# A decoder layer on one core: first weights in halves, the first norm without GpSimd, and additions to x by transfers

## The chip, the core and the metric

The kernel runs on one core of a Trainium2 chip. Five engines work side by side: TensorE (PE, matrix products into PSUM), VectorE (DVE), ScalarE (ACT), GpSimd (POOL) and SyncE (SP, which only issues transfers). Transfers run on 16 DMA engines. The metric is the device time of one execution in microseconds; the time of a kernel is the median of its runs.

## The reference

One decoder layer in float32, 512 tokens by 1024 channels:

```python
x = x + 0.5 * swiglu(rms_norm(x, g_ffn1), w_ffn1_gate, w_ffn1_up, w_ffn1_down)
h = rms_norm(x, g_mix)
q, k, v, u, mq = split(h @ w_in)
# sliding-window attention, conv module, cross-attention into 256 memory tokens
x = x + concat([y_attn, y_conv, y_mem]) @ w_out
x = x + 0.5 * swiglu(rms_norm(x, g_ffn2), w_ffn2_gate, w_ffn2_up, w_ffn2_down)

def rms_norm(x, g):
    return x * rsqrt(mean(x * x, axis=-1) + 1e-6) * g
def swiglu(x, w_gate, w_up, w_down):
    return (silu(x @ w_gate) * (x @ w_up)) @ w_down
```

The hidden width of each feed-forward block is 2816.

## The kernel before

x stays in on-chip memory, transposed: `x[:, d]` is channel block d (128 channels on the partitions, 512 tokens along each), d = 0 to 7. A hidden tile f (0 to 21) is 128 hidden channels.

**Products.** Each float32 product is made of three matmuls over rounded parts (`mm3`, lines 337 to 339): high part of the weights by high part of the data, high by low, low by high. So each weight tile and each data tile is split first: ScalarE copies it to the rounded type (`whi`, `xh`, `hh`), and VectorE subtracts that from the original (`wlo`, `xl`, `hl`). `Weights` does this for the weights: `load_to` issues the transfer of a 128x1024 tile from SyncE (line 140) into one of four raw buffers, `split_to` makes its parts (lines 165 and 166), a few tiles ahead of their use. A raw buffer is free for the next load when its parts are made.

**The start.** The first two tiles (gate and up of hidden tile 0) and x come in pieces, so that TensorE can begin early. `STARTS` names groups of channel blocks; for each group SyncE issues the group's x and, for both weights, the columns that belong to it (`load_piece`, line 173). Further on, for each group, `scaled_split` (lines 348 and 349) makes xh and xl, and `split_piece` (lines 177 and 178) makes the parts of the weights. Eleven matmuls on zeros (line 298) run on TensorE before the first data are there.

**The norm.** The products of hidden tile 0 do not wait for the norm: its factor is applied to the results. `Norm.add(d)` squares `x[:, d]` and adds it to a running sum; `Norm.stats` sums over the partitions on TensorE (line 373) and takes the reciprocal root; `spread` makes the factor `rb` that later instructions multiply by. In the first norm the squares of blocks 0 to 3 are made on GpSimd (line 360) and those of 4 to 7 on ScalarE (line 362); GpSimd adds them up (line 366), except for the last, which VectorE adds (line 368). The two later norms square on ScalarE and add on GpSimd, the last on VectorE.

**The feed-forward block** (`ffn`). Hidden tiles 0 to 3 are plain products of x; for them `blocks` also prepares x for the later ones (`bh`, `bl`). Tiles 4 to 21 use a scheme with seven block products in place of eight (`fast`, lines 439 to 441). The way down to x goes in six rounds of hidden tiles (`ROUNDS`). Round 0 covers tiles 0 to 3: for each of the eight channel blocks, 12 matmuls into a PSUM bank, and one VectorE instruction that adds half of it to x:

```python
DVE.scalar_tensor_tensor(o, ps, 0.5, xd, op0=ALU.mult, op1=ALU.add)
```

Six of these eight steps stand ahead of hidden tile 4, the other two within hidden tile 5. The rounds after it follow in later hidden tiles; round 1's first step stands in hidden tile 8 or after. Both feed-forward blocks run the same function.

`work()` hands out one of five 128x512 buffers named t, which squares, intermediate results of `fast` and others share. PSUM has four banks mm, two sc and two tp. The order of the instructions on each engine is fixed when the program is built: a scheduler takes the program's order and fills an engine's modelled gaps with later instructions that are ready.

Of the kernel before, what the change touches and what calls it, by code (L numbers as in the profile page):

```python
# [34 lines left out]
AF = mybir.ActivationFunctionType  # L35
ALU = mybir.AluOpType
AX = mybir.AxisListType

P = 128
T = 512  # L40
KT = 8
# [8 lines left out]
C_G1, C_GM, C_G2, C_GMEM = 0, 8, 16, 24  # L50
# [5 lines left out]
C_N = C_INVF + 1  # L56


STARTS = [[0], [1], [2, 3], [4, 5], [6, 7]]
N_WARM = 11  # L60


# [124 lines left out]
def per_load(r):  # L187

    return 8 // (ROUNDS[r][1] - ROUNDS[r][0])
# [14 lines left out]
def layer(tc, ctx, a):  # L204
    nc = tc.nc
    PE, ACT, DVE, POOL = nc.tensor, nc.scalar, nc.vector, nc.gpsimd
# [8 lines left out]
    def nm(s):  # L215
        uid[0] += 1
        return f"{s}_{uid[0]}"

    def mm_bank():
        return psum.tile([P, T], F32, tag="mm", name=nm("mm"), bufs=4)  # L220
# [7 lines left out]
    def work():  # L228
        return tmp.tile([P, T], F32, tag="t", name=nm("t"), bufs=5)
# [5 lines left out]
    W = Weights(nc, wpool, dma_ahead=3, conv_ahead=3, bufs=(4, 4))  # L235
# [46 lines left out]
    x = keep.tile([P, KT, T], F32, name="x")  # L282
# [4 lines left out]
    def atile(name, dtype=F32R):  # L287
        return act.tile([P, T], dtype, tag="h", name=nm(name), bufs=N_ACT)
# [10 lines left out]
    W.split_to(2)  # L299
    for ks in STARTS:  # L300
        nc.sync.dma_start(x[:, ks[0] : ks[-1] + 1], a["xT"][:, ks[0] : ks[-1] + 1])
        for i in range(2):
            W.load_piece(i, slice(ks[0] * P, (ks[-1] + 1) * P))
    W.load_to(4)
    nc.scalar.dma_start(ident, a["ident"])

# [27 lines left out]
    def mm3(ps, wh, wl, ks, hi, lo, first, last, woff=0):  # L334
        for i, k in enumerate(ks):
            w = slice((k - woff) * P, (k - woff + 1) * P)
            PE.matmul(ps, wh[:, w], hi(k), start=first and i == 0, stop=False)  # L337
            PE.matmul(ps, wh[:, w], lo(k), start=False, stop=False)  # L338
            PE.matmul(ps, wl[:, w], hi(k), start=False, stop=last and i == len(ks) - 1)  # L339
# [4 lines left out]
    def scaled_split(d, gcol):  # L344

        g = par[:, gcol + d : gcol + d + 1]
        xh[d], xl[d] = atile("xh"), atile("xl")
        ACT.activation(xh[d], x[:, d], AF.Identity, scale=g)
        DVE.scalar_tensor_tensor(xl[d], x[:, d], g, xh[d].bitcast(F32), op0=ALU.mult, op1=ALU.subtract)  # L349

    class Norm:
# [2 lines left out]
        def __init__(self):  # L354
            self.sum = None

        def add(self, d, on_pool=False):
            sq = work() if d else tmp.tile([P, T], F32, tag="sqsum", name=nm("sqsum"), bufs=1)
            if on_pool:
                POOL.tensor_tensor(sq, x[:, d], x[:, d], op=ALU.mult)  # L360
            else:
                ACT.activation(sq, x[:, d], AF.Square)
            if d == 0:
                self.sum = sq
            elif d < KT - 1:
                POOL.tensor_tensor(self.sum, self.sum, sq, op=ALU.add)
            else:
                DVE.tensor_tensor(self.sum, self.sum, sq, op=ALU.add)

        def stats(self):  # L370
            self.ps = tp_bank()
# [17 lines left out]
    def ffn(pool, norm, first, gain, hooks, next_gain, last):  # L389
# [89 lines left out]
        def down(r, g):  # L479

            lo, hi = ROUNDS[r]
            end = r == len(ROUNDS) - 1
            wh, wl = W.next()

            def step(j):
                d = g * per_load(r) + j
                cut = last and end and d == KT - 1
                for t0, t1 in [(0, T // 2), (T // 2, T)] if cut else [(0, T)]:
                    ps = mm_bank()[:, : t1 - t0]
                    mm3(  # L490
                        ps, wh, wl, range(lo, hi), lambda k: h_hi[k][:, t0:t1], lambda k: h_lo[k][:, t0:t1],
                        True, True, woff=lo - j * (hi - lo),
                    )
                    xd = x[:, d, t0:t1]
                    o = work()[:, : t1 - t0] if last and end else xd
                    DVE.scalar_tensor_tensor(o, ps, 0.5, xd, op0=ALU.mult, op1=ALU.add)  # L496
                    if last and end:
                        nc.sync.dma_start(a["out"][d, :, t0:t1], o)
                if end and not last:
                    nxt.add(d)  # L500
                    scaled_split(d, next_gain)

            return [lambda j=j: step(j) for j in range(per_load(r))]
# [42 lines left out]
        r = len(ROUNDS) - 1  # L546
# [5 lines left out]

    norm = Norm()
    for ks in STARTS:
        scaled_split(ks[0], C_G1)
        for i in range(2):
            W.split_piece(i, slice(ks[0] * P, (ks[-1] + 1) * P))
        for k in ks[1:]:
            scaled_split(k, C_G1)
    W.split_to(3)  # L560
    for k in range(KT):
        norm.add(k, on_pool=k < 4)

    mk = keep.tile([P, 2, ML], F32, name="mk")
    mv = keep.tile([P, 2, ML], F32, name="mv")
# [149 lines left out]
    with tc.tile_pool(name="fast1", bufs=1) as pool:  # L715
        norm = ffn(pool, norm, STARTS, C_G1, hooks, C_GM, False)

    with tc.tile_pool(name="mix", bufs=1) as mix:
        norm = mixing(tc, nc, a, mix, W, norm, locals())

    with tc.tile_pool(name="fast2", bufs=1) as pool:
        ffn(pool, norm, [[0, 1, 2, 3, 4, 5, 6], [7]], C_G2, {}, None, True)


def mixing(tc, nc, a, mix, W, norm, e):
# [483 lines left out]
```

## Time and profile before

| | |
|---|---|
| median of 3 runs | 881.68 us (881.55 to 882.0) |
| profiled execution: time, span | 884.32 us, 882.5 us |
| TensorE busy | 871.1 us (99%) |
| VectorE busy | 711.9 us (81%) |
| ScalarE busy | 439.0 us (50%) |
| GpSimd busy | 45.9 us (5%) |
| mean granted TensorE clock | 0.990 |
| HBM read, written | 85.45 MB, 2.10 MB |

The span runs from the first to the last instruction of the profiled execution, which is a run of its own and not among the three of the median. Lines such as L337 are lines of the kernel below. In a row of a group stand the engine, the operation, what it writes and reads (names without buffer numbers), shapes, the count, the busy time and the mean duration, and then the engine's idle time ahead of these instructions and who ended it. In a row in order of time stand the start in us, the duration, engine, line, operation and shapes. A window's row has the busy us and the number of instructions of each engine, the granted clock of TensorE (1.00 is full), the share of the DMA engines and GB/s. The durations of matmuls overlap: their pitch is read from the starts.

### The profile page before, as it was taken

To read this page: it belongs to the slowest core of one execution; us is meant where nothing else is said; L and a number is where in the kernel's file an instruction comes from. 1 tells how busy PE (TensorE), PEld (TensorE's weight loads), DVE (VectorE), ACT (ScalarE), POOL (GpSimd) and SP (SyncE) were. 2 spreads that over 40 slices of the span, in tenths; PEclk is the share of its full clock that TensorE was granted. 3 is DMA by queue.
4 is the path that set the end of the run, shared out by engine and by line. 5 is a ranking of instruction groups with operands and counts; after the bars stand their busy time and mean duration, and the time that the engine had idled before them with its cause. 6 is when DMAs were issued, how large, how long until landed. Compare 5 with 4: busy or idle time off the path is not lost.

```text
span 882.5 us, 14009 instructions
## 1 busy us (share of the span) xinstructions
PE 871.1 (99%) x5509; PEld 761.9 (86%) x5509; DVE 711.9 (81%) x1166; ACT 439.0 (50%) x733; POOL 45.9 (5%) x38
## 2 busy tenths in 40 slices
PE   7999999999999999999999999999999999999998
PEld 3889999899999999888676788889999999989997
DVE  6999978986796886769998876999987778767872
ACT  6354555454563444533937864345554454544540
POOL 6000000000020000300020012000000000000000
PEclk8999999999999999999997999999999999999999
DMA  5522333333334244221010233323334232332312
GB/s 196 167 96 74 118 121 108 106 110 118 118 123 124 92 120 150 72 95 61 1 60 13 69 111 96 96 72 120 98 115 122 83 123 86 118 108 83 115 53 96
DMA packets 34083, 88.46 MB, mean 100 GB/s; under 512 B 3168, under 2 KB 7008, under 8 KB 34016
## 3 DMA queue, kind: packets, MB, share of 16 engines
q1 hardware_dynamic: 32864, 85.99, 30.8%
q10 hardware_dynamic: 1152, 1.57, 0.6%
q8 instruction: 43, 0.70, 0.3%
q14 instruction: 24, 0.20, 0.1%
HBM read 85.45 MB, written 2.10 MB: 99 GB/s over the span
## 4 chain that ended last, share of the span: by engine, by line
PE 91%; DVE 4%; DMA 2%; ACT 1%; issue 1%; DVEq 0%
PE mm L337 15%; PE mm L339 15%; PE mm L338 15%; PE mm L439 10%; PE mm L441 10%; PE mm L440 10%; PE sc L439 2%; PE sc L441 2%; PE sc L440 2%; PE tp L926 1%; PE sc L339 1%; PE sc L337 1%; PE sc L338 1%; PE sc L855 1%; DVE wlo L166 1%
## 5 line engine op out<-in xcount | busy, mean ns | idle before, releaser
L439 PE MATMUL mm<-bh,whi 128*128 128x256 f32 x864 | 239.2, 277 | 0.6 <-ACT kept L450 0.3
L440 PE MATMUL mm<-bl,whi 128*128 128x256 f32 x864 | 238.7, 276 | 0.0
L441 PE MATMUL mm<-bh,wlo 128*128 128x256 f32 x864 | 238.7, 276 | 0.0
L165 ACT CAST whi<-wraw 128x1024 fp32r<-128x1024 f32 (+2 forms) x122 | 124.3, 1022 | 123.5 <-PE mm L338 53.2
L166 DVE TENSOR_TENSOR wlo<-wraw,whi 128x1024 fp32r<-128x1024 f32 (+2 forms) x122 | 145.1, 1190 | 29.0 <-ACT whi L165 28.9
L439 PEld LDWEIGHTS mm<-bh,whi 128*128 128x128 f32 x864 | 162.3, 188 | 2.1 <-ACT kept L450 0.5
L440 PEld LDWEIGHTS mm<-bl,whi 128*128 128x128 f32 x864 | 162.2, 188 | 1.2
L441 PEld LDWEIGHTS mm<-bh,wlo 128*128 128x128 f32 x864 | 162.2, 188 | 0.0
L339 PE MATMUL mm<-hh,wlo 128*128 128x512 f32 (+1 forms) x356 | 139.3, 393 | 0.0
L338 PE MATMUL mm<-hl,whi 128*128 128x512 f32 (+1 forms) x356 | 139.3, 393 | 0.0
L337 PE MATMUL mm<-hh,whi 128*128 128x512 f32 (+1 forms) x356 | 138.6, 392 | 0.0
L166 DVE TENSOR_TENSOR wlo<-s,whi 128x1024 fp32r<-128x1024 f32 x72 | 88.4, 1229 | 30.3 <-ACT whi L165 30.0
L165 ACT CAST whi<-s 128x1024 fp32r<-128x1024 f32 x72 | 75.5, 1050 | 53.1 <-PE mm L440 36.1
L339 PEld LDWEIGHTS mm<-hh,wlo 128*128 128x128 f32 x356 | 66.9, 188 | 15.5
L337 PE MATMUL mm<-xh,whi 128*128 128x512 f32 x192 | 77.5, 406 | 1.6 <-ACT whi L177 1.6
L339 PE MATMUL mm<-xh,wlo 128*128 128x512 f32 x192 | 77.5, 403 | 1.6 <-DVE wlo L178 1.6
L337 PEld LDWEIGHTS mm<-hh,whi 128*128 128x128 f32 x356 | 66.9, 188 | 13.6
L338 PEld LDWEIGHTS mm<-hl,whi 128*128 128x128 f32 x356 | 66.9, 188 | 13.3
L338 PE MATMUL mm<-xl,whi 128*128 128x512 f32 x192 | 76.7, 400 | 1.1 <-DVE xl L349 1.0
L496 DVE SCALAR_TENSOR_TENSOR x<-mm,x 128x512 f32<-128x512 f32 x88 | 59.6, 686 | 10.0 <-PE mm L339 9.9
L460 ACT ACTIVATE t<-t 128x512 f32<-128x512 f32 x36 | 22.8, 632 | 55.5 <-DVE t L459 55.5
L165 ACT CAST vhi<-wraw 128x512 fp32r<-128x512 f32 x36 | 22.3, 621 | 51.8 <-PE sc L440 37.4
(244 smaller groups left out, 1404.3 us busy)
## 6 DMA issues: line engine op xcount, KB each, us to landing
wraw<-in_wgu SPq DMA_DIRECT2D x86, 512.0 KB, 3.5
wraw<-in_wd SPq DMA_DIRECT2D x44, 512.0 KB, 3.7
wraw<-in_win SPq DMA_DIRECT2D x12, 512.0 KB, 3.4
out<-t SPq DMA_DIRECT2D x7, 256.0 KB, 2.0
x<-in_xT SPq DMA_DIRECT2D x3, 512.0 KB, 6.4
wraw<-in_wout_a SPq DMA_DIRECT2D x6, 256.0 KB, 2.6
t<-in_memT ACTq DMA_DIRECT2D x4, 256.0 KB, 3.5
wraw<-in_wmk SPq DMA_DIRECT2D x2, 512.0 KB, 4.0
```

The costliest lines, as they stand in the source:

```text
L165: nc.scalar.copy(hi[:, :cols], raw[:, :cols])
L166: nc.vector.tensor_tensor(lo[:, :cols], raw[:, :cols], hi[:, :cols].bitcast(F32), op=ALU.subtract)
L337: PE.matmul(ps, wh[:, w], hi(k), start=first and i == 0, stop=False)
L338: PE.matmul(ps, wh[:, w], lo(k), start=False, stop=False)
L339: PE.matmul(ps, wl[:, w], hi(k), start=False, stop=last and i == len(ks) - 1)
L439: PE.matmul(ps, wh[:, c], bh[k][:, block], start=one, stop=False, skip_group_check=not first)
L440: PE.matmul(ps, wh[:, c], bl[k][:, block], start=False, stop=False, skip_group_check=not first)
L441: PE.matmul(ps, wl[:, c], bh[k][:, block], start=False, stop=end, skip_group_check=not first)
L460: ACT.activation(g, g, AF.Silu)
L496: DVE.scalar_tensor_tensor(o, ps, 0.5, xd, op0=ALU.mult, op1=ALU.add)
L855: PE.matmul(banks[h][:, i * ML + c.start : i * ML + c.stop], self.q[rows, n * P : (n + 1) * P], self.kt[rows, ks], start=True, stop=True, ...
L926: PE.transpose(ps[:, i * P : (i + 1) * P], self.p[n, h][:, c : c + P], ident)
```

## The change

1. The pieces of the first two weights are halves of 512 columns: the first half with channel block 0, the second with blocks 2 and 3. SyncE's order becomes x0, first halves, x1, x2-3, second halves, x4-5, x6-7, and the parts are made in four instructions on each engine in place of ten.
2. In the first norm all eight squares are made on ScalarE and all sums on VectorE.
3. In round 0 of both feed-forward blocks ScalarE copies half of the PSUM bank into a work buffer, and GpSimd issues a transfer that adds this buffer to x.

```diff
-STARTS = [[0], [1], [2, 3], [4, 5], [6, 7]]
+STARTS = [(0,), (1,), (2, 3), (4, 5), (6, 7)]
+
+PIECES = {(0,): slice(0, 512), (2, 3): slice(512, 1024)}
...
         nc.sync.dma_start(x[:, ks[0] : ks[-1] + 1], a["xT"][:, ks[0] : ks[-1] + 1])
-        for i in range(2):
-            W.load_piece(i, slice(ks[0] * P, (ks[-1] + 1) * P))
+        if ks in PIECES:
+            for i in range(2):
+                W.load_piece(i, PIECES[ks])
...
-        def add(self, d, on_pool=False):
+        def add(self, d, engine=POOL):
             sq = work() if d else tmp.tile([P, T], F32, tag="sqsum", name=nm("sqsum"), bufs=1)
-            if on_pool:
-                POOL.tensor_tensor(sq, x[:, d], x[:, d], op=ALU.mult)
-            else:
-                ACT.activation(sq, x[:, d], AF.Square)
+            ACT.activation(sq, x[:, d], AF.Square)
             if d == 0:
                 self.sum = sq
-            elif d < KT - 1:
-                POOL.tensor_tensor(self.sum, self.sum, sq, op=ALU.add)
             else:
-                DVE.tensor_tensor(self.sum, self.sum, sq, op=ALU.add)
+                (engine if d < KT - 1 else DVE).tensor_tensor(self.sum, self.sum, sq, op=ALU.add)
...
                     xd = x[:, d, t0:t1]
+                    if r == 0:
+                        o = work()
+                        ACT.activation(o, ps, AF.Copy, scale=0.5)
+                        POOL.dma_start(xd, o, accum_op=ALU.add)
+                        continue
                     o = work()[:, : t1 - t0] if last and end else xd
                     DVE.scalar_tensor_tensor(o, ps, 0.5, xd, op0=ALU.mult, op1=ALU.add)
...
     for ks in STARTS:
-        scaled_split(ks[0], C_G1)
-        for i in range(2):
-            W.split_piece(i, slice(ks[0] * P, (ks[-1] + 1) * P))
-        for k in ks[1:]:
+        for k in ks:
             scaled_split(k, C_G1)
+        if ks in PIECES:
+            for i in range(2):
+                W.split_piece(i, PIECES[ks])
     W.split_to(3)
     for k in range(KT):
-        norm.add(k, on_pool=k < 4)
+        norm.add(k, DVE)
```

The later norms call `nxt.add(d)` and keep GpSimd for their sums.

More of the change, by code (lines that the diff above doesn't have):

```diff
@@ L721, in layer @@
     with tc.tile_pool(name="fast2", bufs=1) as pool:
-        ffn(pool, norm, [[0, 1, 2, 3, 4, 5, 6], [7]], C_G2, {}, None, True)
+        ffn(pool, norm, [(0, 1, 2, 3, 4, 5, 6), (7,)], C_G2, {}, None, True)
 def mixing(tc, nc, a, mix, W, norm, e):
```

## The prediction

> **What bounds the kernel now.** I read the page first, then the waits of TensorE, then the first 30 us by windows and in order of time.
>
> ```profile
> span 882.5 us, 14009 instructions
> PE 871.1 (99%) x5509; PEld 761.9 (86%) x5509; DVE 711.9 (81%) x1166; ACT 439.0 (50%) x733; POOL 45.9 (5%) x38
> ...
> PE 91%; DVE 4%; DMA 2%; ACT 1%; issue 1%; DVEq 0%
> ...
> L166 DVE TENSOR_TENSOR wlo<-wraw,whi 128x1024 fp32r<-128x1024 f32 (+2 forms) x122 | 145.1, 1190 | 29.0 <-ACT whi L165 28.9
> ...
> out<-t SPq DMA_DIRECT2D x7, 256.0 KB, 2.0
> ...
> x<-in_xT SPq DMA_DIRECT2D x2, 256.0 KB, 3.6
> ```
>
> TensorE is busy for 871.1 of 882.5 us and holds 91% of the chain that ended last. The only way to a shorter time is to take away what is left of its waiting, so the question is where that is. Its waits from 27 to 880 us (longest and shortest of four):
>
> ```profile
> PE tp L804 <- ACT t L795: 1.8, 1, 1.8
> ...
> PE mm L439 <- ACT kept L454: 0.3, 1, 0.3
> ```
>
> The longest is 1.8 us, in the attention; the shortest are in one hidden tile, far from the edits. So the start is the place: windows of it, then three later ones (busy us of PE, PEld, DVE, ACT, POOL, clock, DMA share, GB/s).
>
> ```profile
> 0.00:4.00 4.00, 2.81 (x7) 1.04 (x8) 0.42 (x6) 1.49 (x2) 0.33 (x5) 1.00 0.53 138
> 4.00:6.00 2.00, 2.00 (x7) 1.01 (x6) 1.16 (x3) 1.11 (x3) 0.91 (x1) 1.00 0.88 218
> 6.00:8.00 2.00, 1.64 (x6) 0.75 (x5) 0.92 (x2) 1.11 (x3) 1.04 (x1) 1.00 0.81 246
> 8.00:10.00 2.00, 1.43 (x5) 0.90 (x5) 0.36 (x2) 0.20 (x1) 0.15 (x1) 1.00 0.90 300
> 10.00:12.00 2.00, 1.00 (x2) 0.37 (x2) 1.44 (x2) 1.98 (x5) 2.00 (x2) 1.00 1.04 392
> 12.00:14.00 2.00, 1.09 (x3) 0.83 (x3) 2.00 (x2) 2.00 (x5) 2.00 (x3) 0.53 1.03 374
> 14.00:16.00 2.00, 2.00 (x6) 1.06 (x5) 2.00 (x3) 2.00 (x6) 1.92 (x2) 0.50 0.83 340
> 16.00:18.00 2.00, 2.00 (x6) 1.60 (x6) 2.00 (x2) 2.00 (x4) 1.92 (x2) 0.50 0.03 12
> ...
> 60.00:70.00 10.00, 10.00 (x45) 8.05 (x44) 10.00 (x15) 4.21 (x6) 0.00 (x0) 1.00 0.14 52
> ...
> 466.10:476.30 10.20, 10.20 (x32) 6.42 (x33) 9.46 (x48) 5.68 (x18) 1.73 (x2) 0.50 0.10 26
> ```
>
> From 10 to 18 us few matmuls start although DMA has delivered nearly everything by 16 us (12 GB/s after it): VectorE and GpSimd are both full there, and the granted clock is 0.50. What VectorE does in it:
>
> ```profile
> 11.36 1.50 DVE L178 TENSOR_TENSOR wlo<-wraw,whi 128x256 fp32r<-128x256 f32 x1
> ...
> 18.77 1.78 DVE L349 SCALAR_TENSOR_TENSOR xl<-x,par,xh 128x512 fp32r<-128x512 f32 x1
> ...
> 21.90 0.74 DVE L349 SCALAR_TENSOR_TENSOR xl<-x,par,xh 128x512 fp32r<-128x512 f32 x1
> ...
> 25.02 0.68 DVE L368 TENSOR_TENSOR sqsum<-sqsum,t 128x512 f32<-128x512 f32 x1
> ```
>
> The same xl takes 1.78 us at 18.77 and 0.74 at 21.90. A 128x256 difference takes 1.50, though one of 128x512 takes 0.68 when GpSimd rests. By group, first 30 us:
>
> ```profile
> L366 POOL TENSOR_TENSOR sqsum<-sqsum,t 128x512 f32<-128x512 f32 x6 | 9.4, 1564 | 0.3
> L349 DVE SCALAR_TENSOR_TENSOR xl<-x,par,xh 128x512 fp32r<-128x512 f32 x8 | 9.1, 1132 | 6.7 <-ACT xh L348 6.7
> ...
> L348 ACT ACTIVATE xh<-x,par 128x512 fp32r<-128x512 f32 x8 | 5.7, 718 | 4.4 <-DMA x<-in_xT 3.5 <-DMA par<-in_par 0.9
> ...
> L362 ACT ACTIVATE t<-x 128x512 f32<-128x512 f32 x4 | 2.4, 620 | 0.0
> ```
>
> GpSimd's six sums cost 9.4 us of its own time and slow VectorE for just as long, and the matmuls of the first tile hang on VectorE. The Trainium skill (SBUF — State Buffer, "Who interferes with whom") says that a VectorE instruction with two SBUF inputs contends with a GpSimd instruction that reads SBUF. The trace agrees: 1.78 against 0.74 us.
>
> **The change part by part: the start.** How far TensorE is by 26.96 us, where the sums of squares enter it:
>
> ```profile
> L338 PE MATMUL mm<-xl,whi 128*128 128x512 f32 x18 | 8.5, 471 | 1.1 <-DVE xl L349 1.0
> L339 PE MATMUL mm<-xh,wlo 128*128 128x512 f32 x17 | 8.2, 480 | 1.6 <-DVE wlo L178 1.6
> L337 PE MATMUL mm<-xh,whi 128*128 128x512 f32 x18 | 8.1, 468 | 1.6 <-ACT whi L177 1.6
> ```
>
> That is 53 matmuls: 48 of hidden tile 0 and five of tile 1. Their pitch at both clocks:
>
> ```profile
> 17.23 0.63 PE L339 MATMUL mm<-xh,wlo 128*128 128x512 f32 x1
> 17.65 0.63 PE L337 MATMUL mm<-xh,whi 128*128 128x512 f32 x1
> ...
> 26.04 0.39 PE L338 MATMUL mm<-xl,whi 128*128 128x512 f32 x1
> 26.27 0.39 PE L339 MATMUL mm<-xh,wlo 128*128 128x512 f32 x1
> ```
>
> 0.42 us at half clock, 0.23 at full. The question is when the 53rd ends after the change.
>
> Arrivals first. One x block or one half of a weight is 0.26 MB. By the GB/s of the windows, 0.55 MB had moved by 4 us, 0.99 by 6, 1.48 by 8, 2.08 by 10, 2.86 by 12, 3.61 by 14, 4.29 by 16. How long after its bytes a transfer is usable:
>
> ```profile
> 6.33 0.72 ACT L348 ACTIVATE xh<-x,par 128x512 fp32r<-128x512 f32 x1 [1.18 <-DMA x<-in_xT]
> ...
> 9.80 0.72 ACT L348 ACTIVATE xh<-x,par 128x512 fp32r<-128x512 f32 x1 [2.37 <-DMA x<-in_xT]
> ```
>
> In the order of issue x1 ends at 0.77 MB (moved at 5.0, used at 6.33) and x2,3 at 1.43 (7.8, used at 9.80): 1.3 to 2.0 us. SyncE now issues nine transfers ahead of the third weight instead of fifteen, in the order x0, both first halves, x1, x2-3, both second halves, x4-5, x6-7. With the parameters and the identity counted that gives: first halves at 5.5 and 7.0 us, x1 at 8.2, x2-3 at 10.7, second halves at 11.5 and 12.0, x4-5 at 13.4, x6-7 at 14.8, the third weight at 16. The halves cost at the front (k=1 comes some 1.9 us later than now) and nothing at the end, since the bytes are the same.
>
> TensorE: k=0 from about 6.2 (first half at 5.5 plus a cast of 0.62, the duration of a square of the same 128x512), k=1 from 8.9, k=2 and 3 from 11.4 to 14.2 as xl2 and xl3 come, k=4 and 5 from about 14.2, and then 24 matmuls of 0.23 are 5.5 us: tile 0 ends at 19.7, and the five of tile 1 at 20.8, if the clock stays full. Now: 26.96. That is 6.1 us.
>
> VectorE: eight xl at 0.74, four half-weight differences and seven sums at 0.68, two 128x1024 differences of 1.19: 15.8 us by durations, and, as a next instruction starts a little before the one ahead has ended, an estimated 14.4. Of it only two xl, two differences and a sum, about 3.1 us, can run before 11.4, because x and weights come no earlier. The other 11.3 end at 22.7. Now the last sum starts at 25.02, and one 128x1024 difference behind it ends the same list near 26.9. That is 4.2 us. ScalarE gets four more squares (4 x 0.62 = 2.5 us) and six fewer casts; it was idle for 4.4 us in its own start and is done by about 19, so only a square that stands ahead of an xh delays something, by at most 0.62 each. GpSimd loses everything in the start.
>
> So TensorE could be 6.1 us ahead and VectorE 4.2. From 60 to 70 us VectorE is busy 10.00 of 10.00 while TensorE also is: how much slack lies between them no row shows. Taken between the two: 5.4 us, nearer to TensorE, since it is the one that never waits; the ends 4.2 and 6.1 stay for the range. Once gained at the start it stays, as no later wait is over 1.8 us. Third and later weights come earlier as well, since their buffers are freed by these differences.
>
> **The clock.** At 12 to 18 us it was 0.50, after windows with 1.43 and 1.00 us of TensorE work in 2. In the new order 8 to 12 us holds about nine matmuls, 2 us in 4: on the edge. If the clock halves for those 24 matmuls, 24 x 0.19 = 4.6 us are lost at most, 2 to 3 if it recovers half-way. The Trainium skill (TensorE: Matmul & The Clock Gate, "What's actually happening") has the gate fall after at least one idle window of about 3.4 us; by that alone the new start, with no such gap, would stay at full clock, and the sum would keep its 6.1. The trace is less kind: it fell here with work in every window.
>
> **The additions to x.** Round 0 of both feed-forward blocks: eight additions on VectorE go, eight copies on ScalarE and eight adding transfers from GpSimd come, 256 KB each.
>
> ```profile
> 69.02 1.29 DVE L496 SCALAR_TENSOR_TENSOR x<-mm,x 128x512 f32<-128x512 f32 x2
> ...
> 77.14 0.69 DVE L496 SCALAR_TENSOR_TENSOR x<-mm,x 128x512 f32<-128x512 f32 x1 [0.27 <-PE mm L339]
> ...
> 84.01 0.69 DVE L459 TENSOR_TENSOR t<-mm,kept 128x512 f32<-128x512 f32 x1
> ...
> 87.05 0.68 DVE L470 TENSOR_TENSOR t<-kept,mm 128x512 f32<-128x512 f32 x1
> ```
>
> VectorE is relieved of 8 x 0.69 = 5.5 us per block, worth nothing as long as TensorE does not wait for it, and up to the 1.9 us by which VectorE lags above, if it does. ScalarE's 8 x 0.62 = 5.0 us lie in an engine that is 50% busy (4.21 of 10 at 60 to 70); the PSUM bank comes free no later. The next user of x is round 1:
>
> ```profile
> L496 DVE SCALAR_TENSOR_TENSOR x<-mm,x x9: 681/687/697, 69.0 to 133.0; 128x512 f32<-128x512 f32 x9
> ```
>
> The ninth, at 133.0, is round 1's first, over 50 us behind. On GpSimd nothing queues behind the transfers but the next one. They hold one of five work buffers (t) each until they land. If one takes D us and they go one by one from 69.7 on, the sixth copy (77.14) needs the first landed, the g of 84.01 the second, the u of 87.05 the third: 69.7 + 3D under 87.05, so D under 5.8 costs nothing. No adding transfer is in the trace; the nearest rows are 256 KB out in 2.0 us and 256 KB in, in 3.6, and an addition reads one stream more: 2.0 to twice 3.6 = 7.2 are the bounds, I take 3.6, nothing lost. The DMA share there is 0.14, so the weights have room. By the Trainium skill (DMA: Bandwidth & Descriptors, "Anatomy of one DMA — SWDGE (gpsimd) path") a 256 KB transfer takes an estimated 2.6 us, which gives the same sum.
>
> **Sum.** 5.4 us off the profiled 882.5 gives a span of 877.1. That execution took 884.32 us in all, 2.6 more than the median of the runs, 881.68; the same difference on the median gives 876.3. Anything within 0.2% (1.8 us) a measurement of this kernel could not tell from no change.
>
> **The rivals.**
> (a) Half clock or a badly placed square in the start: the 24 matmuls lose 2 to 3 us, gain 2 to 4, time about 879. For it: the clock row. Against: more work in 8 to 12 us than now.
> (b) More than forecast: the later dip of the clock (0.50 at 466 to 476 us, 10.2 us) falls differently on the shifted work. At most half of 10.2, 5.1 us, would be regained; with half of that, 873.7. Nothing speaks for a direction.
> (c) Gain undone: VectorE, full at 60 to 70 us, takes over the sums that GpSimd did and TensorE then waits for it by what was gained: 881 to 882. Against: the contention cost VectorE more (9.1 us for eight xl against 8 x 0.74 = 5.9, and 0.8 or more on each slowed piece) than six sums of 0.68 = 4.1.
> (d) Slower: adding transfers over 5.8 us each. Each us more costs 3 us per block through the third work buffer, 6 in both; the 5.4 are gone at D = 6.7, and from 7.0 it is slower by over 1.8 us; at 7.2, 884.7. The Trainium skill (SBUF — State Buffer, "A bandwidth-pool intuition that's wrong (but worth ruling out)") speaks for it: GpSimd cannot write descriptors while a 2-port VectorE instruction runs. Against: the work there is two-input differences, and the nearest transfers take 2.0 to 3.6.
>
> **How the numbers follow.** Forecast 0.62 (gain 4.2 to 6.1 or somewhat more: 875 to 877.5); (a) 0.15; (b) 0.09; (c) 0.06; (d) 0.08. Faster by over 0.2%: 0.62 + 0.15 + 0.09 = 0.86; same 0.06; slower 0.08. The range takes in (a) and most of (b) and leaves out (c) and (d): 872.8 to 879.5.
>
> **What would show it.** Right: xl at about 0.74 in all eight rows; no GpSimd tensor work in the first 25 us; clock 1.00 from 12 to 18 us; the sums of squares entering TensorE near 21 to 22 us; no new TensorE wait from 55 to 110 us and from 590 to 640. Wrong: a row of 0.50 in the start; TensorE waiting for hl, wlo or bl at 50 to 70 us; ScalarE or VectorE waiting for a t buffer until a transfer lands; a weight landing later around the adding transfers.

## Result: 0.5% faster, and what the profile after shows

The changed kernel takes 878.32 us (median of 7 runs, 877.41 to 880.89), the kernel before 882.13 beside it (7 runs, 881.55 to 885.05). The ratio is 0.9948, 95% interval 0.9936 to 0.9961: 3.4 to 5.6 us of 882. (The plain quotient of the two medians is 0.9957, 3.8 us apart, inside that interval.) The forecast was 5.4 us and 876.3. Two executions of the experiments below, one of 2215 us (e5_copy_then_add) and one of 4919 us (e6_idle_gpsimd_work), lie far outside; the medians count them, the ratios do not. The profiled executions are 5.9 us apart in span (882.5 and 876.6). The page of the changed kernel:

```profile
span 876.6 us, 14048 instructions
...
PE 868.4 (99%) x5509; PEld 760.4 (87%) x5509; DVE 697.1 (80%) x1150; ACT 449.2 (51%) x747; POOL 46.3 (5%) x44
...
q0 software_dynamic: 2304, 4.20, 3.0%
...
PE 94%; DVE 2%; ACT 1%; DMA 1%; issue 1%; SPq 0%; ACTq 0%
...
x<-t POOLq DMA_DIRECT2D x16, 256.0 KB, 5.6
```

TensorE is as full as before. New are the queue of the adding transfers (packets, MB, share of the span of 16 DMA engines) and their row: 5.6 us each at the median, not 3.6.

The start by windows, columns as in the prediction:

```profile
8.00:10.00 2.00, 1.94 (x9) 1.14 (x8) 1.31 (x3) 1.20 (x3) 0.00 (x0) 1.00 1.05 415
10.00:12.00 2.00, 1.94 (x8) 1.28 (x9) 2.00 (x4) 2.00 (x5) 0.00 (x0) 1.00 1.03 421
12.00:14.00 2.00, 1.98 (x8) 1.04 (x6) 2.00 (x4) 2.00 (x5) 0.00 (x0) 1.00 0.99 401
14.00:16.00 2.00, 1.54 (x7) 1.27 (x8) 2.00 (x4) 2.00 (x5) 0.00 (x0) 1.00 0.90 338
16.00:18.00 2.00, 2.00 (x10) 1.66 (x9) 2.00 (x4) 2.00 (x4) 0.00 (x0) 1.00 0.46 184
```

Between 10 and 18 us 28 matmuls start; before it was 13 (a window also counts a matmul that began ahead of it). GpSimd does nothing and the clock is 1.00 all through. The eight xl as a group, first 30 us:

```profile
L352 DVE SCALAR_TENSOR_TENSOR xl<-x,par,xh 128x512 fp32r<-128x512 f32 x8 | 6.0, 753 | 4.3 <-ACT xh L351 4.3
```

753 ns each, where it was 1132. In order of time, the end of VectorE's first list and the sums of squares on TensorE:

```profile
19.85 2.51 DVE L168 TENSOR_TENSOR wlo<-wraw,whi 128x1024 fp32r<-128x1024 f32 x2
```

```profile
19.86 0.39 PE L342 MATMUL mm<-xh,wlo 128*128 128x512 f32 x1
...
20.54 0.95 PE L371 MATMUL tp<-ones,sqsum 128*128 128x1 f32 x8
```

The matmul at 19.86 is the 61st of the kernel. The 61st of the kernel before is the row at 26.04 in the prediction: TensorE is 6.18 us ahead. Below, **lead** always means this: how much earlier the matmul of the same number (by start; each kernel has 5509) begins than in the profiled kernel before. The lead after the change runs 6.18 us at 40 us, 5.69 after hidden tile 5, 6.30 after hidden tile 9, 6.37 after the attention and 5.82 at the end. So the gain is made in the first 20 us, and 0.5 us is given back once in each feed-forward block. (The 0.6 us at hidden tile 9 is a pause of the kernel before, which the changed kernel does not have.) Where, in the first block (windows of after, then of before):

```profile
64.00:68.00 4.00, 4.00 (x19) 3.23 (x18) 3.56 (x6) 3.08 (x4) 2.64 (x4) 1.00 0.91 131
68.00:72.00 4.00, 4.00 (x24) 3.46 (x23) 3.35 (x6) 1.88 (x3) 0.86 (x1) 1.00 1.07 309
72.00:76.00 4.00, 4.00 (x38) 4.00 (x37) 2.25 (x2) 2.08 (x4) 0.86 (x1) 1.00 1.08 238
```

```profile
68.00:72.00 4.00, 4.00 (x18) 3.22 (x18) 4.00 (x6) 0.00 (x0) 0.00 (x0) 1.00 0.00 0
72.00:76.00 4.00, 4.00 (x18) 3.20 (x17) 4.00 (x6) 2.10 (x2) 0.00 (x0) 1.00 0.31 93
76.00:80.00 4.00, 4.00 (x32) 3.81 (x31) 3.73 (x6) 1.42 (x2) 0.00 (x0) 1.00 0.23 56
```

In this stage the DMA engines were nearly empty before and are full now (a share of 0.91 to 1.08). What waits for them, 55 to 110 us, of after and then of before (total, times, longest):

```profile
DVE s L126 <- DMA wraw<-in_wgu: 5.2, 3, 2.0
```

```profile
DVE s L124 <- DMA wraw<-in_wgu: 0.2, 1, 0.2
```

A weight load that SyncE issues just in time lands late: the three loads issued from 65 to 74 us take 4.7, 7.3 and 4.8 us to land, where those of the kernel before take 3.4 to 4.3 from 73 to 99 us. From there to TensorE, in order of time (VectorE, ScalarE, TensorE):

```profile
77.92 0.69 DVE L126 TENSOR_TENSOR s<-wraw 128x512 f32<-128x512 f32 x1 [2.04 <-DMA wraw<-in_wgu]
...
80.87 0.69 DVE L457 TENSOR_TENSOR t<-mm,kept 128x512 f32<-128x512 f32 x1
```

```profile
81.59 0.64 ACT L458 ACTIVATE t<-t 128x512 f32<-128x512 f32 x1 [1.69 <-DVE t L457]
...
85.66 0.37 ACT L452 ACTIVATE kept<-mm 128x256 f32<-128x256 f32 x1
```

```profile
85.61 0.28 PE L439 MATMUL mm<-bh,wlo 128*128 128x256 f32 x1
86.08 0.38 PE L437 MATMUL mm<-bh,whi 128*128 128x256 f32 x1 [0.20 <-ACT kept L452]
```

The g addition at 80.87 stood at 84.01 before: it has kept 3.1 of the 6.2 us. ScalarE works in a fixed order, so its SiLU and the copy of a PSUM bank at 85.66 are late, and TensorE, whose pitch there is 0.11 us, starts the next matmul 0.47 after the one ahead of it. The same chain costs 0.5 us near 610 us, in the second block.

### The profile page after: what moved, and what is told of

Same layout as the page of the kernel before. It is cut to its first block, busy times and chain, and to the rows that moved or that the text cites. A ratio compares the mean times of both kernels' runs of the same rounds, so it can differ in the third digit from the quotient of the medians.

```text
span 876.6 us, 14048 instructions
## 1 busy us (share of the span) xinstructions
PE 868.4 (99%) x5509; PEld 760.4 (87%) x5509; DVE 697.1 (80%) x1150; ACT 449.2 (51%) x747; POOL 46.3 (5%) x44
## 4 chain that ended last, share of the span: by engine, by line
PE 94%; DVE 2%; ACT 1%; DMA 1%; issue 1%; SPq 0%; ACTq 0%
PE mm L340 15%; PE mm L341 15%; PE mm L342 15%; PE mm L437 11%; PE mm L438 11%; PE mm L439 11%; PE sc L437 2%; PE sc L438 2%; PE sc L439 2%; PE tp L929 1%; PE sc L342 1%; PE sc L340 1%; PE sc L341 1%; PE sc L858 1%; PE tp L943 1%; DMA x<-in_xT 1%
## 5 line engine op out<-in xcount | busy, mean ns | idle before, releaser
L499 DVE SCALAR_TENSOR_TENSOR x<-mm,x 128x512 f32<-128x512 f32 x72 | 48.7, 684 | 9.0 <-PE mm L342 8.9
```

## Experiments

Theories on record were: A, the gain is GpSimd's contention with VectorE, removed; B, VectorE is relieved by the adding transfers; C, the halves make it; and on the additions, D, the transfers crowd out a weight load, against E, the copies and the fixed order cost it, whatever does the addition. F: TensorE waits for results of a slow GpSimd. Each kernel is compared with the kernel before run beside it (medians 883.57 to 883.82, and 882.13 for the first row). Leads are in us at four places: at 38 us, ahead of the attention, behind it, at the end; negative is late.

| kernel | median us | ratio, 95% | leads |
|---|---|---|---|
| after | 878.32 | 0.9948, 0.9936 to 0.9961 | 6.18, 6.30, 6.37, 5.82 |
| e1_no_adding | 878.06 | 0.9943, 0.9931 to 0.9955 | 6.54, 4.75, 6.25, 6.25 |
| e2_adding_alone | 884.98 | 1.0023, 1.0011 to 1.0034 | 1.19, 0.10, 0.32, -0.53 |
| e3_norm_alone | 878.18 | 0.9947, 0.9934 to 0.9960 | 5.47, 5.17, 5.17, 5.11 |
| e4_halves_alone | 881.87 | 0.9984, 0.9975 to 0.9993 | 1.93, 1.85, 3.07, 3.08 |
| e5_copy_then_add | 877.92 | 0.9929, 0.9915 to 0.9944 | |
| e6_idle_gpsimd_work | 886.08 | 1.0035, 1.0022 to 1.0048 | -2.97, -2.64, -1.13, -1.21 |
| e7_squares_on_gpsimd | 879.02 | 0.9947, 0.9930 to 0.9964 | 6.16, 4.28, 4.28, 4.28 |
| e8_sums_on_gpsimd | 881.04 | 0.9975, 0.9963 to 0.9987 | 4.00, 3.90, 3.67, 2.94 |
| e9_rotary_later | 876.78 | 0.9924, 0.9910 to 0.9938 | 6.59, 6.11, 7.63, 7.64 |
| e10_copy_then_add_2 | 876.18 | 0.9917, 0.9902 to 0.9931 | 7.17, 7.10, 8.61, 7.91 |
| e11_copy_then_add_rotary_later | 877.34 | 0.9932, 0.9917 to 0.9948 | 6.18, 7.00, 8.52, 8.10 |

Executions of the same start differ: the five kernels whose start is that of after lead by 6.18 to 7.17 us. And in the attention the lead grows by 1.2 to 1.5 us in six kernels and not in the others, for a reason of the clock that is shown with e10_copy_then_add_2. A single lead is therefore good to about 1 us, and the ratios decide.

**The parts by themselves.** The change without part 3:

```diff
-                    if r == 0:
-                        o = work()
-                        ACT.activation(o, ps, AF.Copy, scale=0.5)
-                        POOL.dma_start(xd, o, accum_op=ALU.add)
-                        continue
```

> The changed kernel with the old additions to x (one VectorE instruction per step of round 0), halves and norm as changed. Theory A (the gain is made in the start, and the adding transfers only cost): the sums of squares enter TensorE near 20.5 us as in the changed kernel, the two TensorE waits of about 0.5 us behind the transfers (near 86 and 610 us) are gone, and the span is about 1 us under the changed kernel's 876.6, near 875.6; against before a ratio of about 0.992 to 0.994. Theory B (VectorE's relief in round 0 carries part of the gain): TensorE waits appear between 55 and 110 us and the span is over 877.5.

Then the kernel before with part 3 alone (the five lines above added), with part 2 alone (`norm.add(k, DVE)`, all squares on ScalarE), and with part 1 alone (`STARTS`, `PIECES` and their loops).

> The kernel before with the adding transfers alone. Theory A: the start as before (sums of squares at 26.96 us), DMA share near 1.0 while the transfers run, a weight load and with it a VectorE wait of 2 us or more behind them, TensorE waits of about 0.5 us once in each block: 0.5 to 1.5 us slower than before, ratio about 1.001. Theory B: faster than before by 1 us or more.

> The kernel before with the first norm's squares on ScalarE and sums on VectorE alone; the weights still in ten pieces. Theory A (contention between GpSimd and VectorE was the cost): xl at about 0.75 us in all eight rows, sums of squares in TensorE near 21 us, 5 to 6.5 us faster than before, ratio near 0.993. Theory C (the halves carry the gain, by fewer instructions and larger transfers): under 2 us faster, ratio over 0.998.

> The kernel before with the first weights in halves alone; squares and sums on GpSimd as before. Theory A: xl still up to 1.8 us while GpSimd adds, half clock still in the start, within 1.5 us of before, ratio 0.998 to 1.001. Theory C: 4 to 6 us faster, ratio near 0.994.

The norm alone gives 0.53%, all that the three give together (0.52%). The halves alone give 0.16%, and on top of the norm nothing that can be told (0.57% against 0.53%, intervals overlapping). The adding transfers alone make the kernel slower by 0.23%, with an interval clear of 1. B falls, C falls but for its 0.16%, A stands, though the norm alone stayed under A's figure (0.993) and its sums of squares entered TensorE at 23.1 us, not near 21. The groups of the first 30 us, of part 1 alone and then of part 2 alone, show why:

```profile
L352 DVE SCALAR_TENSOR_TENSOR xl<-x,par,xh 128x512 fp32r<-128x512 f32 x8 | 11.8, 1509 | 4.2 <-ACT xh L351 4.2
```

```profile
L349 DVE SCALAR_TENSOR_TENSOR xl<-x,par,xh 128x512 fp32r<-128x512 f32 x8 | 6.0, 748 | 6.2 <-ACT xh L348 6.2
```

The halves bring data earlier, but beside GpSimd's work an xl then takes 1509 ns on average, so VectorE loses what the transfers gained; the clock, too, is at 0.50 for 3.4 us from 18.2 on. Without GpSimd's work an xl takes 748. In the kernel with the transfers alone the wait near 86 us is there too, twice as long as after the full change (its start lies 5 us later):

```profile
90.60 0.28 PE L441 MATMUL mm<-bh,wlo 128*128 128x256 f32 x1
91.57 0.39 PE L439 MATMUL mm<-bh,whi 128*128 128x256 f32 x1 [0.69 <-ACT kept L454]
```

That kernel also tells what the clock was worth. Its start is built as before, but this execution held 1.00 where the profiled kernel before had 0.50:

```profile
14.00:16.00 2.00, 1.51 (x6) 0.86 (x5) 2.00 (x2) 2.00 (x6) 1.84 (x3) 1.00 0.77 315
16.00:18.00 2.00, 0.80 (x2) 0.48 (x3) 2.00 (x3) 2.00 (x4) 1.92 (x2) 1.00 0.01 2
```

It leads by 1.2 us, so the half clock of the profiled kernel before cost about that much of its start: TensorE was waiting for VectorE most of that time anyway. The mean clocks of the other executions agree. Of the 64 executions of the kernel before that ran beside the experiments, 33 have a mean clock of at most 0.992, like the two profiled executions with 6.8 us of half clock in the start (0.990 in the kernel before, 0.992 in e6_idle_gpsimd_work), and take 884.1 us on average; the other 31 have 0.994 or 0.996 and take 883.0. The clock is not the gain: at 0.994 and more the norm alone takes 878.1 us (four executions), the kernel before beside it 883.1 (eleven), a ratio of 0.994.

**Contention or results that come late.** The kernel without adding transfers, with eight products on GpSimd in the start that nothing uses (they go into a buffer that is filled later):

```diff
+    for k in (2, 3, 4, 5):
+        POOL.tensor_tensor(scr, x[:, k], x[:, k - 2], op=ALU.mult)
+        POOL.tensor_tensor(scr, x[:, k], x[:, k - 1], op=ALU.mult)
```

> The changed kernel with the old additions to x, and eight products of x blocks on GpSimd in the start, which write a buffer that nobody reads before it is written anew. Nothing waits for them. Theory A (GpSimd's reads slow VectorE's two-input instructions): xl and the sums that fall beside them take 1.3 to 1.8 us in place of 0.75 and 0.69, sums of squares enter TensorE 4 to 8 us later than without (24 to 28 us), the gain over before shrinks to 0 to 3 us, ratio 0.997 to 1.000. Theory F (the old start was slow because results waited for slow GpSimd squares and sums): nothing changes, sums of squares at 20 to 21 us, ratio about 0.994.

The whole gain is gone and more: 0.35% slower than before, beyond what A had said (0.997 to 1.000), and the sums of squares enter TensorE at 29.7 us, not at 24 to 28. GpSimd's groups, first 30 us, and VectorE's xl and sums in order of time:

```profile
L563 POOL TENSOR_TENSOR mk<-x 128x512 f32<-128x512 f32 x4 | 6.4, 1610 | 0.3
L562 POOL TENSOR_TENSOR mk<-x 128x512 f32<-128x512 f32 x4 | 6.1, 1520 | 9.0 <-DMA x<-in_xT 8.8
```

```profile
19.38 1.75 DVE L352 SCALAR_TENSOR_TENSOR xl<-x,par,xh 128x512 fp32r<-128x512 f32 x1
21.05 1.76 DVE L366 TENSOR_TENSOR sqsum<-sqsum,t 128x512 f32<-128x512 f32 x1
22.73 0.74 DVE L352 SCALAR_TENSOR_TENSOR xl<-x,par,xh 128x512 fp32r<-128x512 f32 x1
23.40 0.68 DVE L366 TENSOR_TENSOR sqsum<-sqsum,t 128x512 f32<-128x512 f32 x1
```

12.5 us of GpSimd work that no one waits for put TensorE 9.5 us behind the same kernel without it (leads of -2.97 and 6.54). Part of it is the clock's: TensorE stood still for 5 us until an xl was there, and from 19.7 to 26.5 us it had the half clock.

```profile
21.18 0.79 PE L341 MATMUL mm<-xl,whi 128*128 128x512 f32 x1 [5.08 <-DVE xl L352]
```

```profile
22.00:24.00 2.00, 2.00 (x6) 1.48 (x6) 2.00 (x3) 0.00 (x0) 0.26 (x1) 0.50 0.00 0
```

Beside GpSimd's work the two VectorE instructions take 1.75 and 1.76 us, right after it 0.74 and 0.68. F falls; this is A, shown. The Trainium skill (SBUF — State Buffer, "Who interferes with whom") states that contention between VectorE instructions with two SBUF inputs and GpSimd instructions that read SBUF; these rows agree with it.

Which half of GpSimd's work it was: the sums alone put back (`norm.add(k)`), and the squares of blocks 0 to 3 alone put back (`norm.add(k, DVE, on_pool=k < 4)`).

> The changed kernel with the old additions to x, all squares on ScalarE, but the sums of the first norm on GpSimd as before (the last on VectorE). Theory A: six GpSimd sums of about 1.6 us overlap with VectorE's xl again, xl up to 1.8 us, sums of squares in TensorE at 24 to 27 us, ratio 0.996 to 0.999. Theory F: the last sum comes late, but hidden tile 0 ends as early as in the changed kernel (TensorE's 48th matmul of data near 19.5 us).

> The changed kernel without its adding transfers, and with the squares of blocks 0 to 3 on GpSimd as in the kernel before; the sums stay on VectorE. Contention theory: the four squares are 4.3 us of GpSimd's time (1101 and 1038 ns each in the kernel before), about half of the 9.0 us of the six sums that GpSimd made in the kernel with its sums on it, which cost about 2.5 us of the start and 3 us of the time. They should cost about half of it if a square contends as a sum does: xl of 1.0 to 1.8 us beside them, start shift -5 to -6, ratio about 0.996. Rival: a square reads the same tile twice and stands in the time in which VectorE waits for data anyway, so it costs nothing: start shift about -6.5, ratio 0.994.

The sums cost 2.5 us of the start (lead 4.00 against 6.54) and about 0.3%, and TensorE's 48th matmul of data starts at 21.6 us, not near 19.5: F falls here as well. The sums of squares came earlier than A had said, at 22.5 us and not 24 to 27. The squares cost no more of the start than executions differ by (lead 6.16 against 6.54), and nothing that the ratio can tell. They slow VectorE too:

```profile
7.47 4.32 DVE L352 SCALAR_TENSOR_TENSOR xl<-x,par,xh 128x512 fp32r<-128x512 f32 x3
```

4.32 us for three xl in a row, where one takes 0.75 elsewhere. But that lies where VectorE without it waits for data (after the change it is busy for 3.58 of the 6 us from 4 to 10). The expectation "half of the cost of the sums" was wrong, its rival right.

**Who pays for the additions to x.** The changed kernel, with the addition made by VectorE behind the same copy on ScalarE:

```diff
-                        POOL.dma_start(xd, o, accum_op=ALU.add)
+                        DVE.tensor_tensor(xd, o, xd, op=ALU.add)
```

> The changed kernel with ScalarE's copies kept, but VectorE adds the copy to x in place of a transfer. Theory D (the transfers crowd the 16 DMA engines, the weights of hidden tile 5 land late, VectorE waits 2 us for them, g and Silu come late, and TensorE waits for ScalarE's copy behind them): the waits of about 0.5 us near 86 and 610 us are gone, TensorE keeps its lead of 6 us or more up to 150 us, ratio to before 0.992 to 0.995. Theory E (the eight extra copies in ScalarE's fixed order make the wait): they stay.

Its profiled execution is the one of 2215 us, so its waits can't be read; the same kernel was run once more.

> The same kernel as the one with copies on ScalarE and additions on VectorE, run once more because one execution of it was disturbed, so that its waits can be read. Theory D (the transfers crowd out the weight load of hidden tile 5 and the cost is theirs): VectorE waits for wraw by no more than 0.3 us between 55 and 110 us, TensorE has no wait of 0.3 us or more at 80 to 92 us nor at 605 to 617, DMA share at 64 to 76 us stays under 0.5, and the ratio is about 0.993 to 0.994. Theory E (the copies and the scheduler's fixed order cost it, whatever does the addition): TensorE's waits of about 0.5 us near 86 and 610 us stay, and the ratio is 0.995.

The ratios of the two are 0.9929 and 0.9917; the second interval lies wholly below that of after, the first overlaps it. Windows and VectorE's wait for weights (55 to 110 us):

```profile
68.00:72.00 4.00, 4.00 (x29) 3.64 (x28) 3.64 (x6) 1.92 (x3) 0.00 (x0) 1.00 0.41 135
72.00:76.00 4.00, 4.00 (x37) 4.00 (x37) 3.57 (x7) 1.90 (x3) 0.00 (x0) 1.00 0.30 119
```

```profile
DVE s L126 <- DMA wraw<-in_wgu: 0.2, 1, 0.2
```

The DMA engines have room, the weight is there (the loads issued from 66 to 76 us land within 3.4 to 3.7 us), and TensorE's waits near 86 and 610 us are gone: the lead stays at 7.17 us from 38 us past hidden tile 5. D is shown, E falls. The two waits add up to 1.04 us of the lead, 0.12%; the ratios differ by 0.2 to 0.3%. That the transfers cost more than 0.12% here is not shown. The start of this execution was 1 us better than that of after, because x2 and x3 arrived 1 us earlier, and that is not the addition's doing; more of the difference is the clock's, as follows.

The attention in the same execution:

```profile
459.90:466.70 6.80, 6.80 (x19) 4.11 (x17) 6.71 (x42) 4.65 (x15) 0.00 (x0) 0.50 0.10 23
466.70:470.20 3.50, 3.50 (x38) 2.52 (x39) 1.95 (x3) 2.02 (x6) 1.86 (x2) 1.00 0.10 34
```

The clock is at 0.50 for 6.8 us, where the prediction's row at 466 us has 10.2. The shorter dip is what the lead gains in the attention (8.61 against 7.10). It came in six of the twelve profiled executions that can be read, with and without the change's parts. In these traces the clock changes in steps: its dips last 3.41, 6.83 or 10.24 us, that is one, two or three times 3.41. All six short dips in the attention begin when 2851 to 2854 matmuls have started, all six long ones when 2839 to 2849 have. So the length goes with where in the work the step falls, and executions of one kernel differ in that; no run here moved the step on purpose.

This bears on the ratios. Among the profiled executions only those with the short dip have a mean clock of 0.996. Five of the six executions of this kernel have it, one of four of e5_copy_then_add, and two of the seven of after. At 0.994 on both sides the ratio to before is 0.994 for both builds, and 0.995 for e1_no_adding and e3_norm_alone, by few executions each; for after the clocks of the runs of before are not on record.

**The wait at hidden tile 9.** The kernel without adding transfers lost 1.8 us of its lead there, and its ratio, 0.9943, just missed A's 0.992 to 0.994. Its longest waits, TensorE's at 150 to 240 us and VectorE's for weights at 90 to 172:

```profile
PE mm L437 <- ACT kept L448: 2.0, 1, 2.0
```

```profile
DVE s L126 <- DMA wraw<-in_wgu: 8.7, 3, 3.8
```

VectorE waits for weights in other kernels too (5.4 us in the kernel before, 6.0 in e10_copy_then_add_2, in the same stretch), so this row alone is not the reason. At this tile the rotary arithmetic of the attention fills VectorE (busy for 21.3 of the 22 us up to 172). It was moved to hidden tile 13, first without adding transfers, then with copies and VectorE's additions:

```diff
-    hooks = {9: [rotary]}
+    hooks = {13: [rotary]}
```

> The changed kernel with the old additions to x, and the rotary tables made in hidden tile 13 in place of 9. Theory G (behind tile 9 VectorE, with the tables' 17 instructions, becomes what TensorE waits for, and takes back 0.6 to 2.8 us of the start's gain): the TensorE waits between 163 and 173 us vanish and none takes their place near 215 to 235 us, span 1 to 2.5 us under the version without the adding transfers, 873.5 to 875, ratio near 0.992. Rival: the wait only moves to hidden tile 13 or 14, same time.

> The two best variants together: copies on ScalarE, additions on VectorE, and the rotary work in hidden tile 13 in place of 9. If the two gains add up: the copies with VectorE's addition are worth 0.2 to 0.3% over the changed kernel, the later rotary 0.2% over the kernel without adding transfers, so ratio about 0.990, span 873 us. If the rotary work costs the same wherever it stands (it filled VectorE at hidden tile 9; at 13 the profile of the kernel with it there lost 1.7 us at 224 to 227 us, against 0.6 to 2.8 at 160 to 175): no faster than with copies alone, ratio 0.9915 to 0.993, and waits of 0.5 to 1.6 us at 220 to 227 us.

At 150 to 240 us the first of the two still has one listed wait, now at 224 us:

```profile
PE mm L437 <- ACT kept L448: 0.8, 1, 0.8
```

The second has none. The first one's lead rises to 7.67 us past tile 9 and falls to 5.93 past tile 13; in the second it goes from 7.44 to 6.82. So G is right on tile 9, and its rival on the rest: the wait moves along with the rotary work, shorter in the listed waits (0.8 against 2.0 us). The work costs something wherever VectorE is near its limit. Against the kernels with the rotary at tile 9 the ratio falls once (0.9943 to 0.9924) and rises once (0.9917 to 0.9932), with overlapping intervals each time: no gain is shown. The versions with VectorE's addition and that with the later rotary lie at 876.2 to 877.9 us and can't be told from one another. The simplest of them, parts 1 and 2 with the copy and VectorE's addition, is faster than the kernel before in both of its runs (medians 877.92 and 876.18 us). Over the changed kernel the two waits, 0.12%, are shown; the rest of its lead is not told apart from the clock's dip and the start.

## Why the prediction was right, point by point

**The start, 4.2 to 6.1 us, taken 5.4: right, nearer to its upper end.** TensorE's own term came out at 6.18 against 6.1. VectorE's list ended at 22.36 against a forecast of 22.7, so its 4.2 was well placed too, but did not bind: TensorE found it far enough ahead until hidden tile 5. Choosing between the two ends was the error, of 0.8 us: the lagging engine's lead was averaged in without a wait of TensorE for it.

**Arrivals: put up to 1.5 us too late in the prediction.** x2 and the second halves as ScalarE takes them up after the change:

```profile
9.16 0.72 ACT L351 ACTIVATE xh<-x,par 128x512 fp32r<-128x512 f32 x1 [0.80 <-DMA x<-in_xT]
...
10.92 1.12 ACT L179 CAST whi<-wraw 128x512 fp32r<-128x512 f32 x2
```

9.16 for x2 (forecast 10.7), 10.92 for the halves (11.5 and 12.0). The step that failed is "by the GB/s of the windows": the curve of the kernel before was kept, but the halves move faster (below). It changed little: VectorE and ScalarE are both full from 10 us on, and VectorE's list ended only 0.3 us ahead of its forecast.

**The contention: right**, and all but the whole gain. One row is misread on the way: the 0.68 us at 25.02 belong to a sum, not to a difference; a 128x512 difference took 0.69 after the change, so nothing hangs on it. **The clock: right**: 1.00 from 12 to 18 us, with 1.54 to 2.00 us of matmul in each 2, and a mean of 0.994 or 0.996 in all seven executions; rival (a) did not come.

**The adding transfers, "I take 3.6, nothing lost": wrong, and the largest miss.** They took 5.6 us at the median, inside the bounds of 2.0 and 7.2, and up to 8.5 in the second block, outside them. The work buffers coped, but not for the reason given. The sum let the transfers "go one by one", so that a D under 5.8 costs nothing. In the trace they overlap: the first six are issued from 63.0 to 72.6 us and land from 66.5 to 78.7, where one by one at 5.6 us they would have needed 34. So rival (d)'s price of 3 us for each us over 5.8 rests on an order that did not come, and that D's median lay just under 5.8 is luck. GpSimd was not held up in issuing either (0.86 us each, 1.01 at most). What failed is "the DMA share there is 0.14, so the weights have room": that is a mean over 10 us that held no transfer of this kind, and the share of the new ones was put at nothing. From the page's queue row, 3.0% of 876.6 us over 16 transfers is 1.6 us of all 16 engines for each, an estimated 10 us for the six that run within 16 us. The late weight cost 0.5 us in each block after the change; the transfers alone cost 0.23%. The prediction did name the sign to look for ("a weight landing later around the adding transfers").

The Trainium skill (DMA: Bandwidth & Descriptors, "Anatomy of one DMA — SWDGE (gpsimd) path") gave an estimated 2.6 us for 256 KB in the prediction; the measured 5.6 us decides.

**Rivals (b) and (c).** (b): the dip of the clock does vary by 1.5 us, but in the profiled pair it was 10.2 us both times. (c): VectorE took over the sums, and behind the start TensorE has no wait that would take the gain back (its listed waits in the feed-forward blocks are 0.3 us at most).

**The number.** 876.3 against 878.32: 0.45 of the 2.0 us is the kernel before, which stood at 882.13 in these runs. The other 1.6 us is the gain, 3.8 between the medians against 5.4 forecast; by the ratio it is 4.6, and its interval (3.4 to 5.6) holds the forecast. The time lies outside the 875 to 877.5 that the forecast itself was given, and inside the whole range because (a) had widened it, whose mechanism did not come: that part is luck. Two terms are known. The adding transfers gave back 1.04 us where nothing was set down for them. And the 5.4 us were reckoned from an execution with the half clock in its start, worth 1.1 to 1.2 us, which about half of the executions of the kernel before do not have.

## To carry to other kernels

Work on an engine that nobody waits for can still set the pace: look at what the same instruction costs beside it and after it, in order of time, before calling it hidden. A transfer that replaces arithmetic can cost more than it saves when a just-in-time load shares its stretch, and the DMA share to check is that of the stretch with the new transfers in it. Moving work off the engine that is full is worth nothing while the bound engine doesn't wait for it: when the additions went back to VectorE, the two waits were gone. And when two kernels lie 0.3% apart, look at the clock of each execution before naming a cause.

## What was not expected of the hardware

The transfers of the first weights. From 4 to 10 us, of before, then of after, of part 2 alone (pieces as before) and of part 1 alone:

```profile
4.00:10.00 6.00, 5.06 (x17) 2.66 (x15) 2.44 (x6) 2.41 (x7) 2.10 (x3) 1.00 0.86 255
```

```profile
4.00:10.00 6.00, 5.53 (x18) 2.47 (x16) 3.58 (x6) 4.44 (x8) 0.00 (x0) 1.00 0.99 352
```

```profile
4.00:10.00 6.00, 5.39 (x17) 3.30 (x15) 2.96 (x7) 3.41 (x9) 0.00 (x0) 1.00 0.89 268
```

```profile
4.00:10.00 6.00, 5.02 (x17) 2.47 (x16) 4.03 (x5) 3.99 (x7) 3.90 (x4) 1.00 1.01 364
```

Pieces of 128 and 256 columns move 255 and 268 GB/s at a share of 0.86 and 0.89, halves of 512 columns 352 and 364 at 0.99 and 1.01: more per share of the engines too (some 300 against 358 GB/s at a full share). The windows hold the x blocks' transfers as well, and whether it is the row's length or the number of transfers that makes it, no run tells apart.

While the adding transfers run, the DMA engines move 131 to 309 GB/s at shares of 0.91 to 1.08, weight loads included, where the loads of the start move 421 at 1.03. Taken by the queue row alone, 0.26 MB in 1.6 us of all 16 engines is an estimated 160 GB/s. Each holds GpSimd for 0.86 us to issue:

```profile
L496 POOL DMA_DIRECT2D x<-t x8: 862/862/1007, 63.0 to 97.7; - x8
...
DMA to landing us min/median/max: 3.3/5.6/7.6
```
